# A two-layer decoder trunk in two-part float32: where the rounded weight parts start, and one pool of small buffers for two

## The chip, the cores and the metric

The kernel runs on one core of one Trainium2 chip. The metric is the device time of one execution in microseconds. TensorE (PE in the profile) multiplies, VectorE (DVE) and ScalarE (ACT) do the elementwise work, GpSimd (POOL) a little of it, and SyncE (SP) issues the loads.

## The reference

One sequence of 256 tokens, 2,048 features, goes through two layers. Layer 0 is a gated MLP that mixes tokens in chunks of 128, layer 1 is attention with forget gates over shared keys and values. Behind each stands a feed-forward network with a causal convolution of width 3. Every matrix is float32.

```python
def reference(x, a_norm, a_w_in, ...):
    h = x
    for l in range(DEPTH):                       # DEPTH = 2, N_A = 1
        if l < N_A:
            h = h + chunked_gmlp(rmsnorm(h, a_norm[l]), ...)        # 2048 -> 2 x 2048 -> 2048
        else:
            h = h + forgetting_attention(rmsnorm(h, b_norm[j]), ...) # q, gate, out: 2048 x 2048 each
        h = h + conv_ffn(rmsnorm(h, f_norm[l]), ...)                # 2048 -> 2 x 5632 -> 2048
        if l == N_A - 1:
            k_sh, v_sh, c_sh = fox_shared_kv(h, ...)                # k, v: 2048 x 2048 each
    return rmsnorm(h, final_norm)
```

## The kernel before, in words

**Two parts.** A product of float32 matrices is made of three products of parts. A weight chunk of 128 x 1024 numbers arrives in a tile `raw`; ScalarE copies it into `whi`, which is rounded to the matmul's float32r format (L82), and VectorE writes what the rounding left, `raw - whi`, into `wlo` (L83). The activations are kept in the same way: for each of 16 (or 44) blocks of 128 features, a row of 512 numbers holds the 256 tokens' rounded parts and then the 256 tokens' rests. They stand in `X1` (norms of h), in `X2` of a phase (`mlp_X2`, `att_X2`, which the profile shows as `mlp_X` and `att_X`) and in `H` of the feed-forward network (`ffn_H`). The profile shows `X1` as `X`.

**Feature-major products** (`feat_block`) have 128 x 128 weights as the stationary operand and the activations as the moving one. For each weight block there is one matmul with a `whi` block over all 512 columns of a row (`mm(ps[:, m, :], w, xx[:, kt, :], ...)`), and one with the `wlo` block over the 256 rounded columns only. A chunk has 8 blocks, 4 rows times 2 outputs (m = 0, 1): 8 matmuls with `whi`, then 8 with `wlo`; the last chunk of an output takes `wlo` first. In the order of the program this gives runs of 8 or 16 alike. The feed-forward networks, the gate and up halves of the two layers (`a_in_u`, `b_g`) and both output projections (`a_out`, `b_out`) are made so: 5,248 matmuls with `whi` and 5,248 with `wlo`.

**Token-major products** (`tok_block`) have a 128 x 128 piece of the activations as the stationary operand and 512 columns of `whi` or `wlo` as the moving one, in threes: rounded activations with `whi`, with `wlo`, then the rests with `whi`. v of layer 0 and q, k, v of layer 1 are made so: 1,536 matmuls. The 16 forget gates (`kvf_f`, function `forget`) are feature-major with 128 x 16 blocks of weights, 32 matmuls in all.

**Order.** `Stream` holds all chunks in the order of the program, 6 loads ahead and 3 splits ahead of the matmuls, and what follows an output (`done`) goes on a few statements per chunk. The four `raw`, four `whi` and four `wlo` buffers rotate. All matmuls come from one helper, so they have one line, L166; the loads are L70.

**Layout.** Bytes within a partition, in the program as it is built: `X1` starts at 36,192 and `mlp_X2`, `att_X2` and `H` at 129,376. All four lie at 96 modulo 256, and each row of 2,048 bytes and each half row keeps that. The `whi` buffers start at 87,968 and the `wlo` buffers at 104,352, each 4,096 long: all at 160 modulo 256, and a 128 x 128 block (512 bytes per partition) keeps that. So in a feature-major product the weights lie 64 bytes past the activations modulo 256, both parts alike.

**Small buffers.** `sq` (2 buffers of 2,048 bytes) takes squares for the norms; `half` (2 buffers of the same size) takes the second half of a PSUM result, before VectorE adds it to the first (`scaled_sum`, L276 and L277).

Of the kernel before, what the change touches and what calls it, by code (L numbers as in the profile page):

```python
# [10 lines left out]
F32 = mybir.dt.float32  # L11
F32R = mybir.dt.float32r
# [5 lines left out]
P = 128  # L18
D = 2048
T = 256  # L20
# [4 lines left out]
CHUNK = 1024  # L25
EPS = 1e-6
SCALE = 128 ** -0.5
AHEAD = 3
LOADS = 6
NEG = -3e38  # L30


# [7 lines left out]
class Stream:  # L40
# [4 lines left out]
        self.items, self.pending = [], []  # L45
        self.raw, self.parts = {}, {}

    def chunk(self, src, mult, at_load=None, at_split=None):
        self.items.append((src, mult, at_load, at_split))

    def then(self, at_load=None, at_split=None, at_mult=None):
        self.items.append((None, at_mult, at_load, at_split))

    def start(self, gen):
        self.pending.append(gen)
# [4 lines left out]
                self.pending.remove(g)  # L60

    def _load(self, i):
        src, _, at_load, _ = self.items[i]
        if at_load:
            at_load()
        if src is None:
            return
        raw = self.pool.tile([P, CHUNK], F32, name="raw", tag="raw", bufs=LOADS - AHEAD + 1)
        raw = raw[:, :src.shape[1]]
        self.nc.sync.dma_start(raw, src)  # L70
        self.raw[i] = raw

    def _split(self, i):
        if self.items[i][3]:
            self.items[i][3]()
        raw = self.raw.pop(i, None)
        if raw is None:
            return
        n = raw.shape[1]
        hi = self.pool.tile([P, CHUNK], F32R, name="whi", tag="whi")  # L80
        lo = self.pool.tile([P, CHUNK], F32R, name="wlo", tag="wlo")
        self.nc.scalar.activation(hi[:, :n], raw, AF.Copy)  # L82
        self.nc.vector.tensor_tensor(lo[:, :n], raw, hi[:, :n].bitcast(F32), op=OP.subtract)  # L83
        self.parts[i] = (hi, lo)

    def run(self):
        n = len(self.items)
        for i in range(-LOADS, n):
            if 0 <= i + LOADS < n:
                self._load(i + LOADS)  # L90
            if 0 <= i + AHEAD < n:
# [41 lines left out]
def build(ctx, tc, d, out):  # L133
# [4 lines left out]
    small = ctx.enter_context(tc.tile_pool(name="small", bufs=1))  # L138
# [13 lines left out]
    s = Stream(nc, wpool)  # L152
    ph = Phase(tc)

    def main_ps():
        return psum.tile([P, 2, 512], F32, name="ps", tag="ps", bufs=3)
# [4 lines left out]
    def column(i):  # L161
        return col[:, i:i + 1]
# [5 lines left out]
    def feat_block(src, x, K, done):  # L168

        box = {}  # L170
        n = K // 4
        for c in range(n):
            def mult(hi, lo, c=c):
                if c == 0:
                    box["ps"] = main_ps()
                ps, xx = box["ps"], x()
                parts = (hi, lo) if c < n - 1 else (lo, hi)
                for i, part in enumerate(parts):
                    for j in range(4):
                        kt = 4 * c + j  # L180
                        for m in range(2):
                            w = part[:, j * 256 + m * P:j * 256 + (m + 1) * P]
                            if part is hi:
                                mm(ps[:, m, :], w, xx[:, kt, :], kt == 0, kt == K - 1)
                            else:
                                mm(ps[:, m, :T], w, xx[:, kt, :T], False, False)
                if c == n - 1:
                    s.start(done(ps))
            s.chunk(src[c], mult)

    def tok_block(src, x, done, load=None, prep=None):

        box = {}
        cuts = [(c, 0, 2) for c in range(8)]
        if prep:
            cuts[:1] = [(0, 0, 1), (0, 1, 1)]
        for c, j0, nj in cuts:
            def mult(hi, lo, c=c, j0=j0, nj=nj):
                kt0 = 2 * c + j0
                if kt0 == 0:  # L200
                    box["ps"] = main_ps()
                ps, xx = box["ps"], x()
                for j in range(nj):
                    kt = kt0 + j
                    w = slice(j * 512, (j + 1) * 512)
                    for tb in range(2):
                        a = xx[:, kt, tb * P:(tb + 1) * P]
                        b = xx[:, kt, T + tb * P:T + (tb + 1) * P]
                        mm(ps[:, tb, :], a, hi[:, w], kt == 0, False)
                        mm(ps[:, tb, :], a, lo[:, w], False, False)  # L210
                        mm(ps[:, tb, :], b, hi[:, w], False, kt == KD - 1)
                if kt0 + nj == KD:
                    s.start(done(ps))
            s.chunk(src[c][:, j0 * 512:(j0 + nj) * 512], mult,
                    load and c and (lambda c=c: load(c)), prep and c and (lambda c=c: prep(c)))


# [44 lines left out]
        nc.scalar.activation(rB, token_rows()[:, :T], AF.Copy)  # L262

    def square_into_acc(p, eng=nc.vector):
        sq = small.tile([P, 2, T], F32, name="sq", tag="sq", bufs=2)
        nc.scalar.activation(sq, h[:, 2 * p:2 * p + 2, :], AF.Square)
        if p == 0:
            eng.tensor_tensor(acc, sq[:, 0, :], sq[:, 1, :], op=OP.add)
        else:
            for i in range(2):  # L270
                eng.tensor_tensor(acc, acc, sq[:, i, :], op=OP.add)

    def scaled_sum(ps, a):

        t = small.tile([P, 2, T], F32, name="half", tag="half", bufs=2)
        nc.scalar.activation(t, ps[:, :, T:], AF.Copy)  # L276
        nc.vector.tensor_tensor(a, ps[:, :, :T], t, op=OP.add)  # L277
        nc.vector.tensor_tensor(a, a, rB[:, None, :].to_broadcast([P, 2, T]), op=OP.mult)  # L278
# [15 lines left out]
    def final(p, gain):  # L294

        def done(ps):
            kts = (2 * p, 2 * p + 1)
            sq = small.tile([P, 2, T], F32, name="sq", tag="sq", bufs=2)
            for m, kt in enumerate(kts):
                nc.vector.tensor_tensor(h[:, kt, :], h[:, kt, :], ps[:, m, :T], op=OP.add)  # L300
                nc.vector.tensor_tensor(h[:, kt, :], h[:, kt, :], ps[:, m, T:], op=OP.add)
                nc.scalar.activation(sq[:, m, :], h[:, kt, :], AF.Square)
            for kt in kts:
                nc.scalar.activation(h[:, kt, :], h[:, kt, :], AF.Copy, scale=column(gain + kt))
            if p == 0:
                nc.vector.tensor_tensor(acc, sq[:, 0, :], sq[:, 1, :], op=OP.add)
            elif p < 7:
                for i in range(2):
                    nc.vector.tensor_tensor(acc, acc, sq[:, i, :], op=OP.add)
            else:  # L310
                token_sums(sq)
                mp = token_rows()
                for a, b in ((0, 2), (2, 6), (6, 11), (11, 16)):
                    nc.vector.tensor_tensor(h[:, a:b, :], h[:, a:b, :],  # L314
                                            mp[:, None, :T].to_broadcast([P, b - a, T]), op=OP.mult)
                    nc.sync.dma_start(out[:, a:b, :], h[:, a:b, :])
            yield
        return done
# [38 lines left out]
    def v_done(blk):  # L357
        def done(ps):
            _, vt, _, _, ss = mlp_kept()
            for tb in range(2):  # L360
                vv = vt[:, tb, blk * 512:(blk + 1) * 512]
                nc.scalar.activation(vv, ps[:, tb, :], AF.Gelu, scale=rcol[:, tb:tb + 1])
                sq = small.tile([P, 2, T], F32, name="sq", tag="sq", bufs=2)
                nc.scalar.activation(sq.rearrange("p a b -> p (a b)"), vv, AF.Square,
                                     accum_out=ss[:, tb, blk:blk + 1])
                yield
            if blk == 3:
                v = small.tile([P, 2], F32, name="ts_v", tag="ts_v", bufs=2)
                rv = ph.keep("rv", [P, 2])
                nc.vector.tensor_reduce(v, ss, axis=AX.X, op=OP.add)  # L370
                nc.vector.tensor_scalar(v, v, 1.0 / D, EPS, op0=OP.mult, op1=OP.add)
                rsqrt(rv, v, 2)
                for tb in range(2):
                    nc.vector.tensor_scalar(vt[:, tb, :], vt[:, tb, :], rv[:, tb:tb + 1], None, op0=OP.mult)
        return done
# [75 lines left out]
    def head_norm(key, blk, gain):  # L451

        def done(ps):
            dst = att(key)
            for tb in range(2):
                x = ps[:, tb, :]
                sq = small.tile([P, 2, T], F32, name="sq", tag="sq", bufs=2).rearrange("p a b -> p (a b)")
                nc.scalar.activation(sq, x, AF.Square, scale=rcol[:, tb:tb + 1])
                v = ph.temp("hv", [P, 4])
                r = ph.temp("hr", [P, 4])  # L460
# [177 lines left out]
    s.then(at_mult=lambda: s.start(kv_operand()))  # L638
    for blk in range(4):
        tok_block(d["b_q"][8 * blk:8 * blk + 8], lambda: X1, head_norm("q", blk, C_QNORM))  # L640
    s.chunk(d["kvf_f"], forget)
    for blk in range(4):
        tok_block(d["kvf_k"][8 * blk:8 * blk + 8], lambda: att("X2"), head_norm("k", blk, C_KNORM))
    s.then(at_mult=lambda: s.start(heads()))
# [69 lines left out]
```

## Time and profile before

| | |
|---|---|
| median of 3 runs | 2249.75 us (2249.28 to 2250.73) |
| the profiled execution's own time | 2249.42 us |
| its span, first to last instruction | 2247.7 us |
| PE, DVE, ACT, POOL busy | 99%, 68%, 53%, 2% of the span |
| granted TensorE clock | 0.997 |
| HBM read | 417.88 MB, 187 GB/s over the span |

A row of a group gives the number of instructions and the mean duration of one. Matmuls are pipelined: the next one starts before the last one's recorded end, so durations of PE rows add up to more than the time they cover. The time from one start to the next, called the spacing in the text, is what adds up.

### The profile page before, as it was taken

Reading aid. Unit: us, or ns where it says so; the run is one execution under the profiler, and the core shown is the slowest. Engines: PE = TensorE matmul, PEld = TensorE weight load, DVE = VectorE, ACT = ScalarE, POOL = GpSimd, SP = SyncE. Lnnn points to the kernel's source line nnn. Section 1 sums busy time; section 2 is a strip of 40 time slices with the busy share of each in tenths; the row PEclk is TensorE's granted clock in tenths of the full one; section 3 lists DMA queues with packets and bytes.
Section 4 is the critical chain, followed back from the end, with each engine's and each line's share of the span. In section 5 each row is a group of like instructions: output and inputs, shape, how many; then the busy total and the mean of one; then the engine's idle time right before and its main releaser. Section 6 shows DMA issues by size and latency. Waiting matters only on the chain.

```text
span 2247.7 us, 32221 instructions
## 1 busy us (share of the span) xinstructions
PE 2227.7 (99%) x12440; PEld 1920.1 (85%) x12440; DVE 1530.0 (68%) x2212; ACT 1190.9 (53%) x1622; POOL 34.7 (2%) x56
## 2 busy tenths in 40 slices
PE   8999999999999999999999999999999999999997
PEld 6888888888888888888788888888888888888886
DVE  6576677777777755557786567677777777765554
ACT  6544455555555544445444666446555555554442
POOL 3000000000000000000000110000000000000000
PEclk9999999999999999999999999999999999999998
DMA  7565555555555655555555555555555556555553
GB/s 281 186 189 172 191 191 192 189 189 194 190 190 190 191 181 193 197 188 177 171 185 188 167 164 185 181 197 188 189 191 192 189 192 191 190 185 197 189 192 116
DMA packets 116442, 422.11 MB, mean 188 GB/s; under 512 B 13232, under 2 KB 13376, under 8 KB 116032
## 3 DMA queue, kind: packets, MB, share of 16 engines
q1 hardware_dynamic: 115344, 417.93, 56.7%
q0 software_dynamic: 768, 2.10, 0.4%
q8 instruction: 97, 1.59, 0.3%
q14 instruction: 57, 0.47, 0.1%
q10 hardware_dynamic: 176, 0.02, 0.0%
HBM read 417.88 MB, written 2.11 MB: 187 GB/s over the span
## 4 chain that ended last, share of the span: by engine, by line
PE 98%; DVE 1%; ACT 0%; DMA 0%; issue 0%; SPq 0%; DVEq 0%
PE ps L166 96%; PE mp L388 0%; PE mp L472 0%; PE mp L558 0%; DMA raw<-a_in_v 0%; PE mp L573 0%; DVE wlo L83 0%; PE mp L581 0%; PE mp L582 0%; PE mp L557 0%; PE mp L580 0%; DVE X L222 0%; DVE h L314 0%; PE mp L244 0%; ACT whi L82 0%
## 5 line engine op out<-in xcount | busy, mean ns | idle before, releaser
L83 DVE TENSOR_TENSOR wlo<-raw,whi 128x1024 fp32r<-128x1024 f32 (+1 forms) x786 | 954.1, 1222 | 381.5 <-ACT whi L82 380.1
L82 ACT ACTIVATE whi<-raw 128x1024 fp32r<-128x1024 f32 (+1 forms) x786 | 821.8, 1054 | 383.7 <-PE ps L166 346.7
L166 PE MATMUL ps<-X,whi 128*128 128x512 f32 x3328 | 829.6, 396 | 0.0
L166 PEld LDWEIGHTS ps<-X,whi 128*128 128x128 f32 x3328 | 602.3, 188 | 120.7
L166 PEld LDWEIGHTS ps<-X,wlo 128*128 128x128 f32 x3328 | 426.0, 188 | 28.3
L166 PE MATMUL ps<-X,wlo 128*128 128x256 f32 x3328 | 430.7, 277 | 0.0
L166 PE MATMUL ps<-ffn_H,whi 128*128 128x512 f32 x1408 | 354.0, 395 | 0.0
L166 PEld LDWEIGHTS ps<-ffn_H,whi 128*128 128x128 f32 x1408 | 252.7, 188 | 48.5
L276 ACT ACTIVATE half<-ps 128x512 f32<-128x512 f32 x104 | 62.3, 599 | 256.0 <-PE ps L166 256.0
L166 PEld LDWEIGHTS ps<-ffn_H,wlo 128*128 128x128 f32 x1408 | 184.3, 188 | 14.5
L166 PE MATMUL ps<-ffn_H,wlo 128*128 128x256 f32 x1408 | 186.4, 277 | 0.0
L277 DVE TENSOR_TENSOR ffn_a<-ps,half 128x512 f32<-128x512 f32 x88 | 60.9, 692 | 175.3 <-ACT half L276 175.3
L166 PE MATMUL ps<-whi,X 128*128 128x512 f32 x512 | 163.6, 397 | 5.8 <-ACT whi L82 5.8
L166 PE MATMUL ps<-whi,att_X 128*128 128x512 f32 x512 | 168.0, 400 | 0.0
L422 DVE SCALAR_TENSOR_TENSOR ffn_c<-ffn_a,col,ffn_c 128x255 f32<-128x255 f32 x352 | 162.0, 481 | 6.3
L418 ACT ACTIVATE ffn_c<-ffn_a,col 128x256 f32<-128x256 f32 x176 | 96.4, 595 | 47.3 <-DVE ffn_a L278 47.3
L166 PEld LDWEIGHTS ps<-whi,X 128*128 128x128 f32 x512 | 97.0, 189 | 26.3 <-ACT whi L82 5.8
L166 PEld LDWEIGHTS ps<-whi,att_X 128*128 128x128 f32 x512 | 96.2, 188 | 20.5
L166 PE MATMUL ps<-wlo,X 128*128 128x512 f32 x256 | 100.9, 394 | 1.3 <-DVE wlo L83 1.3
L166 PE MATMUL ps<-wlo,att_X 128*128 128x512 f32 x256 | 100.1, 391 | 0.0
L221 ACT ACTIVATE X<-h,col 128x256 fp32r<-128x256 f32 x64 | 29.0, 500 | 101.8 <-DVE h L285 99.5
L226 ACT ACTIVATE ffn_H<-ffn_c 128x256 fp32r<-128x256 f32 x88 | 36.8, 418 | 70.0 <-DVE ffn_c L426 70.0
(140 smaller groups left out, 1223.4 us busy)
## 6 DMA issues: line engine op xcount, KB each, us to landing
raw<-up SPq DMA_DIRECT2D x352, 512.0 KB, 3.7
raw<-down SPq DMA_DIRECT2D x176, 512.0 KB, 3.9
raw<-a_in_u SPq DMA_DIRECT2D x32, 512.0 KB, 3.5
raw<-a_out SPq DMA_DIRECT2D x32, 512.0 KB, 3.9
raw<-b_q SPq DMA_DIRECT2D x32, 512.0 KB, 4.2
raw<-kvf_k SPq DMA_DIRECT2D x32, 512.0 KB, 3.5
raw<-kvf_v SPq DMA_DIRECT2D x32, 512.0 KB, 3.8
raw<-b_g SPq DMA_DIRECT2D x32, 512.0 KB, 3.3
```

The source lines that it names most:

```text
L82: self.nc.scalar.activation(hi[:, :n], raw, AF.Copy)
L83: self.nc.vector.tensor_tensor(lo[:, :n], raw, hi[:, :n].bitcast(F32), op=OP.subtract)
L166: nc.tensor.matmul(o, a, b, start=start, stop=stop, skip_group_check=True)
L221: nc.scalar.activation(dst[:, kt, :T], h[:, kt, :], AF.Copy, scale=g)
L226: nc.scalar.activation(dst[..., :T], src, AF.Copy)
L276: nc.scalar.activation(t, ps[:, :, T:], AF.Copy)
L277: nc.vector.tensor_tensor(a, ps[:, :, :T], t, op=OP.add)
L418: nc.scalar.activation(c[:, m, :], a[:, m, :], AF.Identity, scale=w[2], bias=column(C_CONVB + l * 2 * KF + f))
L422: nc.vector.scalar_tensor_tensor(c[:, m, n:], a[:, m, :T - n], w[k], c[:, m, n:], op0=OP.mult, op1=OP.add)
```

## The change

It moves where `whi` starts, and pays for the room with a buffer.

- The buffers of `whi` and `wlo` become 256 bytes longer (`PAD`, 64 numbers), 4,352 bytes. A place per chunk tells where in its buffer each part starts. In feature-major chunks, those of `kvf_f` among them, `whi` starts 44 numbers (176 bytes) into its buffer, which is 80 modulo 256; `wlo` starts at 0, still 160 modulo 256. The activations still start at 96. So `whi` lies 240 bytes past the activations modulo 256 (which is 16 before them), and `wlo` 64 past them as it did.
- In token-major chunks both parts start at 0: 160 modulo 256, as before.
- `sq` and `half` share one rotation of three buffers (tag `tmp`) in place of two each. The 2,048 bytes that this frees are the 8 times 256 bytes of the padding, so everything that comes behind in memory lies where it lay.

On each engine the same instructions stand in the same order as before.

```diff
+PAD = 64
+FEAT_PLACE = (44, 0)
+TOK_PLACE = (0, 0)
...
-    def chunk(self, src, mult, at_load=None, at_split=None):
-        self.items.append((src, mult, at_load, at_split))
+    def chunk(self, src, mult, place, at_load=None, at_split=None):
+        self.items.append((src, mult, at_load, at_split, place))
...
-        hi = self.pool.tile([P, CHUNK], F32R, name="whi", tag="whi")
-        lo = self.pool.tile([P, CHUNK], F32R, name="wlo", tag="wlo")
+        hi, lo = (self.pool.tile([P, CHUNK + PAD], F32R, name=k, tag=k)[:, at:at + CHUNK]
+                  for k, at in zip(("whi", "wlo"), self.items[i][4]))
...
-            s.chunk(src[c], mult)
+            s.chunk(src[c], mult, FEAT_PLACE)
...
-            s.chunk(src[c][:, j0 * 512:(j0 + nj) * 512], mult,
+            s.chunk(src[c][:, j0 * 512:(j0 + nj) * 512], mult, TOK_PLACE,
...
-        sq = small.tile([P, 2, T], F32, name="sq", tag="sq", bufs=2)
+        sq = small.tile([P, 2, T], F32, name="sq", tag="tmp", bufs=3)
...
-        t = small.tile([P, 2, T], F32, name="half", tag="half", bufs=2)
+        t = small.tile([P, 2, T], F32, name="half", tag="tmp", bufs=3)
...
-    s.chunk(d["kvf_f"], forget)
+    s.chunk(d["kvf_f"], forget, FEAT_PLACE)
```

The four other places that take a `sq` are changed in the same way.

More of the change, by code (lines that the diff above doesn't have):

```diff
@@ L46, in __init__ @@
         self.raw, self.parts = {}, {}
-    def chunk(self, src, mult, at_load=None, at_split=None):
-        self.items.append((src, mult, at_load, at_split))
+    def chunk(self, src, mult, place, at_load=None, at_split=None):
+        self.items.append((src, mult, at_load, at_split, place))
     def then(self, at_load=None, at_split=None, at_mult=None):
-        self.items.append((None, at_mult, at_load, at_split))
+        self.items.append((None, at_mult, at_load, at_split, None))
     def start(self, gen):
@@ L62, in _load @@
     def _load(self, i):
-        src, _, at_load, _ = self.items[i]
+        src, _, at_load, _, _ = self.items[i]
         if at_load:
@@ L297, in done @@
             kts = (2 * p, 2 * p + 1)
-            sq = small.tile([P, 2, T], F32, name="sq", tag="sq", bufs=2)
+            sq = small.tile([P, 2, T], F32, name="sq", tag="tmp", bufs=3)
             for m, kt in enumerate(kts):
@@ L362, in done @@
                 nc.scalar.activation(vv, ps[:, tb, :], AF.Gelu, scale=rcol[:, tb:tb + 1])
-                sq = small.tile([P, 2, T], F32, name="sq", tag="sq", bufs=2)
+                sq = small.tile([P, 2, T], F32, name="sq", tag="tmp", bufs=3)
                 nc.scalar.activation(sq.rearrange("p a b -> p (a b)"), vv, AF.Square,
@@ L456, in done @@
                 x = ps[:, tb, :]
-                sq = small.tile([P, 2, T], F32, name="sq", tag="sq", bufs=2).rearrange("p a b -> p (a b)")
+                sq = small.tile([P, 2, T], F32, name="sq", tag="tmp", bufs=3).rearrange("p a b -> p (a b)")
                 nc.scalar.activation(sq, x, AF.Square, scale=rcol[:, tb:tb + 1])
```

## The prediction, as it was put on record

> **What bounds the kernel now.** I read the page first: its busy shares, and the chain of waits that ended last.
>
> ```profile
> span 2247.7 us, 32221 instructions
> PE 2227.7 (99%) x12440; PEld 1920.1 (85%) x12440; DVE 1530.0 (68%) x2212; ACT 1190.9 (53%) x1622; POOL 34.7 (2%) x56
> PE 98%; DVE 1%; ACT 0%; DMA 0%; issue 0%; SPq 0%; DVEq 0%
> ```
>
> TensorE is never out of work for long. The list of waits, longest first, says the same: of those in which PE is the one that waits for a weight part, these are the largest, and they are all at the start.
>
> ```profile
> PE ps L166 <- ACT whi L82: 5.8, 1, 5.8
> PE ps L166 <- DVE wlo L83: 1.3, 3, 0.4
> ```
>
> So the time is the number of matmuls times their spacing. The chain in order of time gives the spacing over long stretches; the first two rows below are the two feed-forward networks, the third one output of the u product, the fourth a piece of q.
>
> ```profile
> 295.76 726.57 PE ps L166 x4184
> 1511.08 721.08 PE ps L166 x4160
> 137.94 11.11 PE ps L166 x64
> 1028.51 16.50 PE ps L166 x72
> ```
>
> Feature-major: 726.57 / 4184 = 173.65 ns, 721.08 / 4160 = 173.34 ns, 11.11 / 64 = 173.6 ns. Half of them have `whi` (512 columns), half `wlo` (256), so a pair costs 347 ns. With 5,248 pairs that is 5,248 x 0.347 = 1,821 us, 81% of the span. Token-major: 16.50 / 72 = 229.2 ns for 512 columns.
>
> To part the pair I read a timeline of PE within one output.
>
> ```profile
> 498.05 2.02 PE L166 MATMUL ps<-X,whi 128*128 128x512 f32 x8
> 499.92 1.07 PE L166 MATMUL ps<-X,wlo 128*128 128x256 f32 x8
> 500.83 2.02 PE L166 MATMUL ps<-X,whi 128*128 128x512 f32 x8
> 502.69 1.98 PE L166 MATMUL ps<-X,wlo 128*128 128x256 f32 x16
> 504.51 0.62 PE L166 MATMUL ps<-X,whi 128*128 128x512 f32 x2
> ```
>
> From start to start, 16 matmuls with `whi` take (499.92 - 498.05) + (502.69 - 500.83) = 3.73 us, 233 ns each. The 24 with `wlo` take 0.91 + 1.82 = 2.73 us, 114 ns each. The same 512 columns cost 229 ns in the token-major row above: there the weights move and the activations stand still, so the two reads lie differently to each other. The groups by shape sharpen this.
>
> ```profile
> L166 PE MATMUL ps<-X,whi 128*128 128x512 f32 x3328 | 829.6, 396 | 0.0
> L166 PE MATMUL ps<-ffn_H,whi 128*128 128x512 f32 x1408 | 354.0, 395 | 0.0
> L166 PE MATMUL ps<-mlp_X,whi 128*128 128x512 f32 x256 | 63.8, 395 | 0.0
> L166 PE MATMUL ps<-att_X,whi 128*128 128x512 f32 x256 | 63.7, 395 | 0.0
> L166 PE MATMUL ps<-X,wlo 128*128 128x256 f32 x3328 | 430.7, 277 | 0.0
> L166 PE MATMUL ps<-wlo,att_X 128*128 128x512 f32 x256 | 100.1, 391 | 0.0
> L166 PE MATMUL ps<-att_X,whi 128*16 128x512 f32 x16 | 5.7, 393 | 0.0
> L558 PE MATMUL mp<-att_k,att_q 128*128 128x256 f32 x32 | 9.6, 380 | 0.0
> ```
>
> A mean duration of 395 goes with a spacing of 233, and 276 to 277 with 114: the duration is the spacing and about 162 ns. With that I turn durations into spacings. The stages' 512-column means are alike although `X1`, `H` and the two `X2` lie far apart; what they share is the 64 bytes modulo 256. Within a group the durations are not alike, as the answer for the tile `ffn_H` (least, median, largest) shows.
>
> ```profile
> L166 PE MATMUL ps<-ffn_H,whi x1408: 388/395/398, 772.6 to 2231.8; 128*128 128x512 f32 x176
> L166 PE MATMUL ps<-ffn_H,wlo x1408: 276/276/281, 774.5 to 2230.0; 128*128 128x256 f32 x176
> ```
>
> With the same 512 columns and no engine to wait for, a matmul spaces 226 ns at the least and 236 at the most. So 5 to 10 ns of the mean of 233 is a stall within TensorE. Its weight load runs beside each matmul and is the one other large reader tied to it.
>
> **The change part by part.**
>
> *Place of `whi`.* The feature-major matmuls with `whi`, 5,248, get another distance between the weights being loaded and the columns being streamed: 240 in place of 64. One nanosecond of spacing is 5.25 us. No row shows 240, so I bound it. The mean is 395.3: the pair's 347.3 ns less 114 for `wlo`, and the 162. From below: the q.k matmul L558, duration 380, spacing 218, which is the shortest of any that keeps PE about as long: 15.3 ns less, 5,248 x 0.0153 = 80 us saved. The next bounds are rows of the same form: the least `ffn_H` duration, 388, spacing 226: 7.3 ns, 38 us saved; and the token-major `wlo` group at another distance (192), mean 391, spacing 229: 4.3 ns, 23 us saved. From above: the largest, 398, spacing 236: 2.7 ns more, 14 us lost. I take the middle of the two rows of the same form, 389.5: 395.3 - 389.5 = 5.8 ns, 5,248 x 0.0058 = 30 us saved. Those two are steady states that this kernel shows with weight loads of full size beside the matmul, whereas L558 multiplies plain float32, with 256 columns.
>
> The Trainium skill, "TensorE: Matmul & The Clock Gate", section "Wait — 56ns, not 53.3ns?", gives a warm spacing of columns / 2.4 GHz and about 2.5 ns, here 216 ns for 512 columns. By it an estimate would be 5,248 x 17 ns = 89 us saved if every stall went; no 512-column row here is that short.
>
> *Place of `wlo`.* Unchanged at 64, as are the token-major chunks: 0. The matmul that stands at a change of parts loads the other part: a small share, taken in the mean.
>
> *The forget gates* (16 matmuls with `whi`): under 0.2 us either way.
>
> *The split.* ACT writes and DVE reads `whi` at another offset. I cost it at nothing, and the cover is this: in the feed-forward network DVE is busy 484.16 of 700 us.
>
> ```profile
> 300.00:1000.00 700.00, 700.00 (x4042) 609.74 (x4041) 484.16 (x643) 377.61 (x493) 0.00 (x0) 1.00 0.58 190
> L83 DVE TENSOR_TENSOR wlo<-raw,whi 128x1024 fp32r<-128x1024 f32 x783 | 952.4, 1225 | 380.7 <-ACT whi L82 379.3
> L82 ACT ACTIVATE whi<-raw 128x1024 fp32r<-128x1024 f32 x783 | 820.2, 1056 | 383.7 <-PE ps L166 346.7 <-issue 9.8 <-DMA raw<-a_in_v 7.4
> ```
>
> A chunk lasts 8 x 0.347 = 2.78 us on PE and costs DVE 1.23 us for the split. A split slower by a fifth would still be 3 chunks ahead. Above that each extra 0.1 us per chunk on a full DVE would be 783 x 0.1 = 78 us; I see no reason for it.
>
> *Three buffers for four.* In the feed-forward network only `half` is live.
>
> ```profile
> L276 ACT ACTIVATE half<-ps x104: 588/599/604, 110.3 to 1988.1; 128x512 f32<-128x512 f32 x104
> L277 DVE TENSOR_TENSOR ffn_a<-ps,half x88: 691/692/693, 296.8 to 1988.8; 128x512 f32<-128x512 f32 x88
> ```
>
> One is written per output, every 11.1 us, and read out 0.6 + 0.7 us later, so even one buffer would do. `sq` and `half` are never wanted within the same output, and `sq` itself has three in place of two. Cost 0. If a buffer came back late, ACT's next split would queue behind the waiting write, and PE would notice only after the three chunks of lead, 8.3 us.
>
> **Sum.** 2249.4 (the profiled execution, 1.7 us of which lie outside its span) - 30 = 2219 us. That execution is 0.3 us under the median, which the rounding covers.
>
> **The rivals.**
>
> *The stall goes nearly all* (the low bound). Spacing 218 to 224, 47 to 80 us saved: 2169 to 2202. For it: L558. Against it: the forget gates load only 16 columns and still have a mean of 393, so most of the stall does not come from how long the load reads. Chance 0.14.
>
> *No change.* Then place modulo 256 is not what sets the stall: 2245 to 2254, in short 2249. For it: the starts of the forget gates, whose weights step 64 bytes per row and so pass four distances modulo 256.
>
> ```profile
> 1108.03 0.40 PE L166 MATMUL ps<-att_X,whi 128*16 128x512 f32 x1
> 1108.38 0.40 PE L166 MATMUL ps<-att_X,whi 128*16 128x512 f32 x1
> 1108.73 0.40 PE L166 MATMUL ps<-att_X,whi 128*16 128x512 f32 x1
> 1109.08 0.39 PE L166 MATMUL ps<-att_X,whi 128*16 128x512 f32 x1
> 1109.43 0.40 PE L166 MATMUL ps<-att_X,whi 128*16 128x512 f32 x1
> 1109.78 0.39 PE L166 MATMUL ps<-att_X,whi 128*16 128x512 f32 x1
> ```
>
> Their distances are 64, 128, 192, 0, 64 and 128. The two at 128 differ, 0.40 and 0.39, so the duration does not follow the distance cleanly. Against it: the token-major rows at distance 192 are steadily 4 ns shorter. Chance 0.10. The Trainium skill, same page, section "Part 2: What happens when you issue a matmul", speaks for this rival: TensorE has two independent read ports, and "Loading the next tile's weights doesn't steal SBUF read bandwidth from the running matmul." By that rule the sum is 2249; the spread from 388 to 398 within one form does not sit well with it.
>
> *Slower: the new distance holds the worst state.* 240 is 16 bytes before the activations, so load and stream begin almost at the same place modulo 256. If that makes every matmul the 398 kind (spacing 236, as about half are now), the price is 14 us: 2263. It decides from a mean `whi` duration of 396.2, where the loss passes 4.5 us. For it: the largest duration is common already at 64, and nothing in this trace shows what 240 does. Against it: the forget gate's row nearest to 240, distance 0 at 1109.08, is a short one, 0.39. Chance 0.20.
>
> That the change doesn't do what it says is hardly open: the layout fixes the addresses, and the buffers of all phases lie where they lay.
>
> **How the numbers follow.** Forecast 0.56 (spacing 224 to 231, 2202 to 2238), nearly all gone 0.14, no change 0.10, slower 0.20. What this kernel's measurement can tell from no change is about 0.2%, 4.5 us. Faster by more: 0.56 + 0.14 = 0.70; same 0.10; slower 0.20. The likeliest case's own range is 2202 to 2238. To reach 8 in 10, the range goes down to 2182, into the first rival (0.05 left out), and up to 2262, nearly all of the slower one (0.08 left out).
>
> **What would show it.** In the profile after, the four `whi` groups should have means of 388 to 391 instead of 395 to 396, the `wlo` groups 276 to 277 as before, the token-major groups 391 to 400 as before. The long pieces of the chain should show (227.5 + 114) / 2 = 171 ns per matmul. The tiles `half` and `sq` should add no wait of PE. I am wrong if the `whi` means stay at 395 (place does not matter), rise above 396 (worst state), fall under 386 (the first rival), or if the time moves while these means do not, which would point at the split or the shared buffers.

## The result, and the profile after

| | before | after |
|---|---|---|
| median of the runs | 2249.98 us (2249.28 to 2250.73) | 2240.99 us (2240.65 to 2241.15) |
| profiled execution's span | 2247.7 us | 2239.4 us |
| ratio of the times | | 0.996, 95% interval 0.9948 to 0.9972 |

The change is 9 us faster. The forecast was 30 us, 2219 us; its sign was right and its size was not. 2241 us lies 3 us over the 2202 to 2238 us of the likeliest case, in the gap between it and no change.

The page after looks like the page before: same shares, same chain.

```profile
span 2239.4 us, 32221 instructions
PE 2219.4 (99%) x12440; PEld 1931.0 (86%) x12440; DVE 1529.9 (68%) x2212; ACT 1187.6 (53%) x1622; POOL 35.0 (2%) x56
PE 98%; DVE 1%; DMA 0%; issue 0%; SPq 0%; DVEq 0%; ACT 0%
```

The long pieces of the chain show where the time went: 723.19 / 4184 = 172.8 ns per matmul in the first feed-forward network, and 172.5 in the second, against 173.65 and 173.34. The token-major piece is unchanged, 229.2 ns.

```profile
295.12 723.19 PE ps L169 x4184
1505.92 717.69 PE ps L169 x4160
1024.49 16.50 PE ps L169 x72
```

The groups by shape show that two things moved, against each other. Columns: count, busy us, mean ns of one.

```profile
L169 PE MATMUL ps<-X,whi 128*128 128x512 f32 x3328 | 817.3, 392 | 0.0
L169 PE MATMUL ps<-ffn_H,whi 128*128 128x512 f32 x1408 | 349.1, 392 | 0.0
L169 PE MATMUL ps<-X,wlo 128*128 128x256 f32 x3328 | 437.5, 279 | 0.0
L169 PE MATMUL ps<-ffn_H,wlo 128*128 128x256 f32 x1408 | 189.0, 279 | 0.0
```

The `whi` groups fell from 395 and 396 to 392. The `wlo` groups rose from 277 to 279, although `wlo` and the activations are where they were. Taken from start to start over all feature-major matmuls of the two traces (those behind a wait left out), `whi` gave 19.1 us back and `wlo` took 10.1 us: together 9.0 us, the whole difference.

A timeline of PE in the same output as before shows how `wlo` lost it.

```profile
498.34 1.10 PE L169 MATMUL ps<-X,wlo 128*128 128x256 f32 x8
499.29 2.00 PE L169 MATMUL ps<-X,whi 128*128 128x512 f32 x8
501.12 1.98 PE L169 MATMUL ps<-X,wlo 128*128 128x256 f32 x16
502.94 3.81 PE L169 MATMUL ps<-X,whi 128*128 128x512 f32 x16
```

The first run of `wlo` takes (499.29 - 498.34) / 8 = 119 ns each, the second one 1.82 / 16 = 114 ns. The second is what nearly all were before; in the following a `wlo` run at 117 to 119 is called wide, and one at 113 to 114 narrow. Two short windows of the groups view show, for each of the two, the last `whi` matmul ahead (x1) and the `wlo` run.

```profile
L169 PE MATMUL ps<-X,wlo 128*128 128x256 f32 x8 | 1.1, 281 | 0.0
L169 PE MATMUL ps<-X,whi 128*128 128x512 f32 x1 | 0.4, 388 | 0.0
...
L169 PE MATMUL ps<-X,wlo 128*128 128x256 f32 x16 | 2.0, 276 | 0.0
L169 PE MATMUL ps<-X,whi 128*128 128x512 f32 x1 | 0.4, 398 | 0.0
```

A `whi` run that ended on a short matmul (388, spacing 226) has a wide `wlo` run behind it (281); one that ended on a long matmul (398, spacing 236) has a narrow one (276). From 100 us on that pairing has no exception: all 253 `whi` runs that ended on a spacing of 225 or 226 had a wide `wlo` run behind them, and all 259 that ended on 233 to 236 a narrow one. Seven ended on 229 or 230, with 3 wide runs behind. The start-to-start times, run by run, are a cycle of four that repeats through the feed-forward networks (ns, from the trace):

```
whi   229 226 229 229 229 226 229 236    entered from a wide wlo run
wlo   118 114 113 113 114 113 113 114    narrow
whi   233 238 233 229 227 226 227 226    entered from a narrow wlo run
wlo   118 117 118 117 119 117 118 118    wide
```

Before, nearly all runs had one form: 226 236 231 236 231 236 231 236 for `whi`, 118 113 114 113 113 114 113 113 for `wlo`. But six of the 519 `wlo` runs were wide there too, with nothing moved. Each of the six stood behind a `whi` run whose second matmul started late (315 to 424 ns after the first; 24 runs have such a start) and which ended on 231. The 513 narrow ones stood behind ends of 233 to 236. A short window of the groups view of before shows one of the six.

```profile
L166 PE MATMUL ps<-X,wlo 128*128 128x256 f32 x7 | 1.0, 281 | 0.0
L166 PE MATMUL ps<-X,whi 128*128 128x512 f32 x1 | 0.4, 393 | 0.0
```

### The profile page after: what moved, and what is told of

Its sections match the earlier page's. It is cut to its first block, busy times and chain, and to the rows that moved or that the text cites. A ratio compares the mean times of both kernels' runs of the same rounds, so it can differ in the third digit from the quotient of the medians.

```text
span 2239.4 us, 32221 instructions
## 1 busy us (share of the span) xinstructions
PE 2219.4 (99%) x12440; PEld 1931.0 (86%) x12440; DVE 1529.9 (68%) x2212; ACT 1187.6 (53%) x1622; POOL 35.0 (2%) x56
## 4 chain that ended last, share of the span: by engine, by line
PE 98%; DVE 1%; DMA 0%; issue 0%; SPq 0%; DVEq 0%; ACT 0%
PE ps L169 96%; PE mp L391 0%; DVE X L225 0%; PE mp L475 0%; DMA raw<-a_in_v 0%; PE mp L561 0%; PE mp L576 0%; DVE wlo L86 0%; PE mp L584 0%; PE mp L585 0%; PE mp L560 0%; PE mp L583 0%; DVE h L317 0%; PE mp L247 0%; PE mp L257 0%
## 5 line engine op out<-in xcount | busy, mean ns | idle before, releaser
L169 PE MATMUL ps<-X,whi 128*128 128x512 f32 x3328 | 817.3, 392 | 0.0
L169 PEld LDWEIGHTS ps<-X,wlo 128*128 128x128 f32 x3328 | 431.5, 188 | 25.7
L169 PE MATMUL ps<-X,wlo 128*128 128x256 f32 x3328 | 437.5, 279 | 0.0
L169 PE MATMUL ps<-ffn_H,whi 128*128 128x512 f32 x1408 | 349.1, 392 | 0.0
```

What stands on the lines that cost most here:

```text
L169: nc.tensor.matmul(o, a, b, start=start, stop=stop, skip_group_check=True)
```

## The experiments

Two theories stood at the start. A: the distance between weights and activations modulo 256 sets the spacing, and a run hands a state on to the run behind it. B: the shared buffers, the longer tiles or the place of a tile by itself explain part of the 9 us or of the missing 21. In the sums below, each part's change of mean spacing (from start to start) is multiplied by 5,248.

### The pooling alone

```diff
-FEAT_PLACE = (44, 0)
+FEAT_PLACE = (0, 0)
```

> Both parts start at 0 (64 past the activations, as before); the padding and the three shared buffers stay. Theory A (the distance between weights and activations sets the spacing, the shared buffers do nothing): 2249.5 to 2250.5 us, no change; whi groups mean 395 to 396, wlo 276 to 277. Rival B (the shared buffers or the longer tiles brought part of the 9 us, or cost part of the 30 that were forecast): the time moves from before by over 2 us, or the wlo groups rise to 279 as after the change.

Measured: 2249.61 us, ratio 0.9999 (0.999 to 1.0008).

```profile
L169 PE MATMUL ps<-X,whi 128*128 128x512 f32 x3328 | 829.6, 396 | 0.0
L169 PE MATMUL ps<-X,wlo 128*128 128x256 f32 x3328 | 430.7, 277 | 0.0
```

Both groups are those of before. The buffers and the padding cost nothing and bring nothing; the place of `whi` does all of it.

### The same distance another way

Here `whi` starts another 256 bytes further, in a tile padded by 512, and `wlo` is not padded.

```diff
-FEAT_PLACE = (44, 0)
+FEAT_PLACE = (108, 0)
...
-        hi, lo = (self.pool.tile([P, CHUNK + PAD], ...)[:, at:at + CHUNK]
-                  for k, at in zip(("whi", "wlo"), self.items[i][4]))
+        hi, lo = (self.pool.tile([P, CHUNK + pad], ...)[:, at:at + CHUNK]
+                  for k, at, pad in zip(("whi", "wlo"), self.items[i][4], (2 * PAD, 0)))
```

> whi another 256 bytes further (432 bytes into a buffer padded by 512), wlo unpadded at 0: distances 240 and 64 modulo 256 as in the changed kernel, 496 and 64 modulo 512. Theory A (period 256): 2240 to 2242 us, whi 392, wlo 279. Rival (the period is 512 or longer): another value, 2225 to 2265, with other means.

Measured: 2240.70 us, ratio 0.996 (0.9947 to 0.9972). And here activations and weights move together by 96 bytes:

```diff
+    const.tile([P, 24], F32, name="shift")
     X1 = const.tile([P, KD, 2 * T], F32R, name="X1")
...
+    const.tile([P, 40], F32, name="fill")
...
-    small.tile([P, 56], F32, name="place")
+    small.tile([P, 16], F32, name="place")
...
-FEAT_PLACE = (44, 0)
-TOK_PLACE = (0, 0)
+FEAT_PLACE = (4, 24)
+TOK_PLACE = (24, 24)
```

> The activations are moved by 96 bytes to 192 modulo 256, and the weights with them: whi at 176, wlo at 0, token-major parts at 0. All distances are those of the changed kernel (240, 64, 192), all addresses differ by 96. Theory A (the distance sets it): 2240 to 2242 us, whi 392, wlo 279. Rival (the place of the weights or activations by itself, such as whi starting at 80, matters): the time leaves this range by over 3 us.

Measured: 2241.41 us, ratio 0.9962 (0.9948 to 0.9975). In both traces `whi` and `wlo` have the sums of the changed kernel to 0.1 us (19.0 and 19.1 saved, 10.1 and 10.1 lost). It is the distance that counts, and adding 256 bytes changes nothing. Half of that is no period: in the map below, distance 112 has a `whi` mean of 232.9 where 240 has 229.5.

### Both parts at 240

```diff
-FEAT_PLACE = (44, 0)
+FEAT_PLACE = (44, 44)
```

> Both parts start at 44 (240 past the activations). Theory A1 (each part's own distance sets its own spacing, 240 is good for both): whi steady at 226 to 229, wlo at 113 in all runs, time 2221 to 2232. Theory A2 (the state at the end of a run of one part is carried into the run of the other, and the wlo loss comes from that): the wlo runs have states of their own that can't be told beforehand; wlo between 109 and 118, time between 2215 and 2260. Rival B (whi alone matters, the wlo loss is from elsewhere): wlo stays split between 113 and 118, time 2239 to 2243.

Measured: 2256.84 us, ratio 1.0031 (1.0019 to 1.0042), slower than before.

```profile
L169 PE MATMUL ps<-ffn_H,whi x1408: 387/392/398, 775.5 to 2239.7; 128*128 128x512 f32 x176
L169 PE MATMUL ps<-ffn_H,wlo x1408: 278/278/283, 777.4 to 2238.0; 128*128 128x256 f32 x176
```

A1 and the rival both fail. A2 has the time in its wide range, but not `wlo`, whose mean it had at 118 at the most. `whi` saves 20.8 us here, a little more than in the changed kernel, but `wlo` goes 118, 117, 123, 117, 123, 117 in all runs (mean 119.3) and loses 28.0 us. What is good for the 512 columns of `whi` is bad for the 256 of `wlo`.

### A map of distances

`places()` gives each of the 136 feature-major outputs its own pair, and each of the 16 token-major outputs too.

```diff
+def places():
+    n = 0
+    while True:
+        yield (4 * (n % 16), 4 * (n // 16 % 16))        # the second half: n // 16 + 8
+        n += 1
...
-            s.chunk(src[c], mult, FEAT_PLACE)
+            s.chunk(src[c], mult, place)
```

> A map, not a candidate: each feature-major output (136 of them) has its own pair of places, whi at 0, 16, ... 240 bytes and wlo at 0 to 128 bytes; in the token-major outputs both parts move together from 0 to 240 bytes. Theory A: the mean whi spacing of an output depends on the whi place and, through the changes of part, on the wlo place; it repeats for the same pair wherever it lies in the program. It ranges from 224 to 238 and wlo from 109 to 120; total 2225 to 2255 us. Rival (place modulo 256 is not what matters): outputs of all pairs look alike within 1 ns, except by stage.

> The other half of the map: wlo at 128 to 240 bytes (and 0 once more) against all whi places; token-major: whi moves alone, wlo at 0. Theory A: whi at 176 with wlo at 0 gives a mean of 229.6 for whi and 115.9 for wlo as after the change; other pairs range as in the first half, and some pair has both whi under 229 and wlo at 113.5 or less. Total 2225 to 2255 us. Rival: all alike within 1 ns.

Measured: 2274.25 and 2267.15 us, one run each, over the expected 2225 to 2255; 245 of the 256 pairs cost more than the 346.8 ns (232.8 and 113.9) of the kernel before. No pair had both `whi` under 229 and `wlo` at 113.5 or less, as was expected of the second half: the least mean of `wlo` is 114.0. Mean spacings from start to start at ten of the sixteen distances (ns; for `whi` the mean over the sixteen places of `wlo`, for `wlo` the mean over the sixteen places of `whi`):

```
distance      0     16     48     64    112    144    176    192    208    240
whi       229.9  231.2  232.6  233.0  232.9  233.0  230.5  230.4  231.9  229.5
wlo       118.9  118.2  118.1  115.9  119.3  119.0  118.0  117.7  116.8  118.0
```

`whi` is best near 0, at 240 and again at 176 to 192; `wlo` is best at 64, where it had been. The rival (all alike) falls. The column at 64 was not of one kind: beside it, `wlo` was at 114.0 with `whi` at 176 and at 117.8 with `whi` at 112. Since one output is short, two pairs were run whole.

### Two pairs from the map

```diff
-FEAT_PLACE = (44, 0)
+FEAT_PLACE = (32, 0)        # 192; the other kernel: (28, 0), 176
```

> whi at 32 numbers (192 past the activations), wlo at 0 (64). In the map one output with this pair had a pair sum of 344.1 ns against 347.7 for 64/64 and 346.4 for 240/64. Theory A (distances and what is carried from run to run, no more): 5,248 x 3.6 ns = 19 us under before, 2227 to 2235 us, whi means near 392 and wlo means 276 to 278. Rival (one output of the map is no steady state; the carry from run to run makes other values when all outputs are alike): 2236 to 2250.

> whi at 28 numbers (176 past the activations), wlo at 0 (64). In the map two outputs with this pair had 344.4 and 344.8 ns, with wlo at 114, that is without the second, slower state of the wlo runs that the changed kernel has. Theory A: 5,248 x 3.1 ns = 16 us under before, 2230 to 2237 us, wlo means 276 to 277, whi near 392 to 393. Rival: as for e4, 2236 to 2250.

Measured: 2244.96 us, ratio 0.9978 (0.9969 to 0.9988), and 2238.66 us, ratio 0.9951 (0.9938 to 0.9963). Both rivals hold on the time: one output of the map is not the state that many alike settle in. At 192 `whi` saves 13.8 us and `wlo` loses 8.5, with half of its runs wide again. At 176 `whi` saves 12.7, less than at 240, but `wlo` loses only 1.7: all but four `whi` runs in the feed-forward networks end on 235 or 236, and no `wlo` run is wide.

```profile
L169 PE MATMUL ps<-ffn_H,whi x1408: 387/392/398, 769.1 to 2221.4; 128*128 128x512 f32 x176
L169 PE MATMUL ps<-ffn_H,wlo x1408: 276/276/281, 771.0 to 2219.6; 128*128 128x256 f32 x176
```

At 192, 124 of the 257 wide `wlo` runs stand behind ends of 237 or 238. So a wide run does not need a short end: the spacing at the end goes along with the state at 240, but isn't the state itself.

The pair with the worse `whi` (176 against 240) is the faster one: compare the median of `wlo`, 276, with the changed kernel's 280 in the same view.

```profile
L169 PE MATMUL ps<-ffn_H,whi x1408: 387/390/402, 769.8 to 2223.2; 128*128 128x512 f32 x176
L169 PE MATMUL ps<-ffn_H,wlo x1408: 276/280/281, 771.6 to 2221.5; 128*128 128x256 f32 x176
```

### whi without changes of part

The small part is left out of the feature-major products, and the rounded part is multiplied a second time in its place, so that `whi` runs on unbroken; once at 64 (`FEAT_PLACE = (0, 0)`) and once at 240.

```diff
-                for i, part in enumerate(parts):
+                for i in range(2):
...
-                            w = part[:, j * 256 + m * P:j * 256 + (m + 1) * P]
+                            w = hi[:, j * 256 + m * P:j * 256 + (m + 1) * P]
...                                   # one matmul of 512 columns with it each time
```

> Feature-major products leave wlo out and run the whi matmul a second time in its place, at distance 64: whi runs without any change of part. Theory A: 231 and 236 in turn, mean duration 395 to 396, 2 x 5,248 matmuls; about 2249 + 5,248 x 119 ns = 2870 to 2880 us. Rival: without changes of part the spacing at 64 is another one.

> As e9a, at distance 240. Theory A: the steady state alone, 226 to 229, mean duration 389 to 391, so 10,496 x 5 to 6 ns = 52 to 63 us under e9a. Rival (240 saves no more than the 3.3 ns per matmul that the changed kernel shows even in long runs): 35 us under e9a.

Measured: 2878.67 and 2810.04 us, one run each: 68.6 us for 10,496 matmuls, 6.5 ns each. The rows of the tile `ffn_H`, first at 64, then at 240:

```profile
L169 PE MATMUL ps<-ffn_H,whi x2816: 392/396/399, 1003.1 to 2861.3; 128*128 128x512 f32 x188
...
L169 PE MATMUL ps<-ffn_H,whi x2816: 389/389/389, 978.3 to 2792.7; 128*128 128x512 f32 x188
```

Unbroken, 240 settles to 389, where the forecast had put 389.5. Theory A's steady state is there, and is worth more than the 52 to 63 us expected of it; the rival's 35 us falls.

### Fewer changes of part

Every second chunk takes `wlo` first, so that runs of 16 meet; with `whi` at 240, and then at 176.

```diff
-                parts = (hi, lo) if c < n - 1 else (lo, hi)
+                parts = (hi, lo) if c % 2 == 0 and c < n - 1 else (lo, hi)
```

> The changed kernel, but every second chunk takes wlo before whi, so that runs of 16 replace runs of 8: 4 changes of part per output of the feed-forward network's up product in place of 6, about 11 in place of 20 in the down product. Theory A (the distance gives whi its steady 226 to 229, and the loss sits in the changes of part and in the state that a wlo run takes over from the whi run before): of the 2.1 ns by which the whi mean lies over the steady value (11 us), 4 to 6 us go; the wlo runs may go all to 113 (14 us more) or all to 117 (14 us lost), which can't be told beforehand; whi mean 391, time 2222 to 2236, or up to 2250 if wlo locks high. Rival (changes of part don't matter, each part has a fixed spacing at a given distance): 2240 to 2242.

> As e8, with whi at 28 numbers (distance 176), where a change costs little: a whi run starts at 233 instead of 229 and ends in 236, a wlo run of 8 has 118 at both ends. Theory A: with a third fewer changes at about 10 ns each, 330 changes less, 3 to 4 us under the 2238.7 us of e5: 2233 to 2237. Rival (changes don't matter): 2238 to 2240.

Measured: 2239.67 us, ratio 0.9955 (0.9941 to 0.9968), and 2236.34 us, ratio 0.994 (0.9928 to 0.9953). At 240 it brought 1.3 us, 0.3 us past the rival's range: `whi` saves 20.9 us instead of 19.1, 1.8 more where A had 4 to 6, and about half of the `wlo` runs, 172 of 336, are still wide and lose 10.8. At 176 it brought 2.3 us: inside A's range of times, but less than its 3 to 4 us. `wlo` is back at its mean of before.

### Is the state handed on?

At 240, a wide `wlo` run behind a short end was so far a pattern that always held, and no more than a pattern. Here `whi` is at 176, which leaves all `wlo` runs narrow, but for one chunk in four at 240. Nothing is changed about the 240 chunk itself or the `wlo` behind it; only what comes before it is now always a narrow `wlo` run.

```diff
-FEAT_PLACE = (44, 0)
+FEAT_PLACE = (28, 0)
...
-            s.chunk(src[c], mult, FEAT_PLACE)
+            s.chunk(src[c], mult, (44, 0) if c % 4 == 1 else FEAT_PLACE)
```

> whi at distance 176 in all feature-major chunks but every fourth (the second, sixth and tenth of an output), which have 240; wlo at 64 everywhere. At 176 each whi run ended on 236 and each wlo run behind it stayed at 113. At 240 a whi run that comes behind such a wlo run went 233, 238, 233 and ended on 226, with a wlo run at 117 behind it. Theory A (the state is handed on from run to run): now every wlo run behind a 240 chunk is at 117 to 118, all of them and not every second, and every other wlo run at 113; 168 runs of 8 or 16 at 3.4 to 4 ns more make 5 us: 2241 to 2245 us. Rival (240 makes half of the wlo runs slow for a reason of its own, whatever came before): half of the runs behind a 240 chunk slow, or slow ones elsewhere; 2238 to 2241.

Measured: 2241.80 us, ratio 0.9964 (0.9951 to 0.9977). All 168 `wlo` runs behind a 240 chunk are wide, against half in the changed kernel; of the 352 others 3 are. Each of the 168 chunks ended on 225 or 226. A timeline shows one wide run and two narrow ones.

```profile
498.15 1.10 PE L169 MATMUL ps<-X,wlo 128*128 128x256 f32 x8
499.09 2.01 PE L169 MATMUL ps<-X,whi 128*128 128x512 f32 x8
500.94 1.98 PE L169 MATMUL ps<-X,wlo 128*128 128x256 f32 x16
502.75 3.85 PE L169 MATMUL ps<-X,whi 128*128 128x512 f32 x16
506.44 1.08 PE L169 MATMUL ps<-X,wlo 128*128 128x256 f32 x8
507.35 0.87 PE L169 MATMUL ps<-X,whi 128*128 128x512 f32 x3
```

The first run, behind a 240 chunk, has 0.94 / 8 = 118 ns; the two behind 176 chunks have 1.81 / 16 and 0.91 / 8, 113 to 114. The rival falls: what a `wlo` run costs follows from what ran before the run before it. A chunk's place in its output, or the buffer it lies in, does not decide it either. In the changed kernel the up product of the first feed-forward network has three `wlo` runs per output and four chunks for four buffers; the wide run is the middle one in one output, and the outer two are the wide ones in the next, in turn through all 43 outputs between 296 and 770 us.

### The best found

```diff
-FEAT_PLACE = (44, 0)
-TOK_PLACE = (0, 0)
+FEAT_PLACE = (28, 0)
+TOK_PLACE = (48, 48)
...                                   # and the order of e10
```

> e10 (176, 64, runs of 16), and both parts of the token-major chunks at 48 numbers, where activations and weights start alike modulo 256 (distance 0; the map's one output with it had a mean of 227.8 against 229.9 at 192). Theory A: 1,536 x 1 to 2 ns = 1.5 to 3 us under the 2236.3 us of e10: 2233 to 2235. Rival (one output is no steady state, or the clipped mean misleads): 2236 to 2238.

Measured: 2234.46 us, ratio 0.9932 (0.992 to 0.9944), the fastest of all: 6.5 us under the change. The token-major piece of the chain went from 16.50 us to 16.34, 227 ns per matmul; over all token-major matmuls the mean spacing went from 229.4 to 228.0 ns.

```profile
1021.29 16.34 PE ps L169 x72
293.75 721.37 PE ps L169 x4184
```

## Why the prediction was right or wrong

- **What bounds the kernel** was right. PE is the chain, its waits for weight parts are as they were (5.9 and 1.3 us, against 5.8 and 1.3), and 19.1 - 10.1 = 9.0 us of matmul spacing is the whole result. The signs that were named came short of it: `whi` means of 392 where 388 to 391 were to come, 172.8 ns per matmul where 171 was, and `wlo` at 279 where it was to stay at 276 to 277.
- **The step that failed** is one for both terms: spacing was taken as a property of a matmul and its own distance. The matmul at a change of part was called "a small share, taken in the mean", and `wlo` was put at "Unchanged at 64 ...: 0". The runs showed a state that each run takes over from the run before it.
- **The term for `wlo`** (0) missed by 10.1 us, with half of its runs at 117 to 118. The trace of before spoke against the 0 already: a `wlo` run's first matmul had 118 and the rest 113, and six runs were wide throughout at the same distance of 64.
- **The term for `whi`** (30 us) was too large by 11. The steady level was close, 389.5 forecast and 389 in unbroken runs (6.5 ns saved where 5.8 was forecast), which over 5,248 matmuls would be 34 us. But that was partly luck. Of the two "steady states" whose middle was taken, 388 (spacing 226) is none: in the trace of before, 500 of the 527 `whi` runs have it on their first matmul and then go on with 236 and 231. The other, 391, is the least of four token-major groups (391, 394, 397 and 400), so these rows aren't "steadily 4 ns shorter". And the kernel changes part after every 8 or 16 matmuls. At 240 a run entered from a narrow `wlo` run spends its first three at 233, 238, 233 before it settles, and one entered from a wide run ends on 236. The middles of the runs saved 17.6 us, the last ones 2.7, and the first three lost 1.3.
- **The split and the shared buffers** at 0 were right: 2249.61 us with both and no move.
- **The low rival** (stall nearly all gone) did not come: no distance of the map brought a mean `whi` under 226. **The slower rival**, all matmuls in the worst state, was wrong for `whi`; a slower kernel came only when `wlo` was moved too (2256.84 us), and through `wlo`. **No change** is out: the time left 2245 to 2254, and the 68.6 us of the unbroken runs come from the distance alone. The rule of the Trainium skill that was weighed there ("TensorE: Matmul & The Clock Gate", "Part 2: What happens when you issue a matmul"), that loading the next weights takes nothing from the running matmul, does not agree with these runs, in which 6.5 ns of a matmul's spacing hang on where the next weights start.

What stays open is the mechanism inside TensorE: what a run hands to the next, and why 256 columns and 512 columns like different distances. The traces show starts, not the reads.

## What to carry to other kernels

Where PE is the bound and matmuls of one form differ in spacing, as they did here from 226 to 236 ns, the place of stationary and moving operands modulo 256 is worth a map: one execution with another place per output shows where to look. But don't add up the best spacing of each kind of matmul: they pass a state on, so a sum over a mixed sequence has to be taken from that sequence, and a place with a slightly worse steady spacing can win because it leaves its neighbours alone (176 against 240). A group whose instructions weren't touched belongs into the sum if it stands next to one that was.

## What the runs showed of the hardware that was not expected

The spacing of a matmul of 512 columns goes through short cycles that repeat to a nanosecond or so: 231, 236 at distance 64 (and 233, 233, 234 in one long stretch of the unbroken run there); 226, 227, 227 or 226, 229, 229, 229 at 240; 226, 229, 236, 229 at 176. A run of 256 columns at distance 64 has two kinds, with means of about 113 and 117.5 ns, and after its first two matmuls keeps the one it is in, up to 16 matmuls on. And the effect depends on the difference of addresses so strictly that moving everything by 96 bytes, or one operand by 256, gave the same sums to 0.1 us.
